# One expert-layer kernel: two of its weight blocks loaded in 16 transfers of eight partitions each

## The chip, the core and the metric

The kernel runs on one core of a Trainium2 chip. A core has TensorE (PE; its weight loads, PEld, overlap its matmuls), VectorE (DVE), ScalarE (ACT), GpSimd (POOL) and SyncE (SP). SP computes nothing here: it issues transfers between HBM and the on-chip memory of 128 partitions, which 16 DMA engines carry out. The metric is the device time of one execution in microseconds.

## What is computed

A layer over 256 latent tokens and 256 context tokens, all of width 1024: a token mixer (a recurrent part and a pooling part), then a mixture of 32 experts, of which each token takes four. Cut to what matters here:

```python
logits = (h @ router_w + router_b)
top_v, top_i = lax.top_k(logits, TOP_K)                # 4 of 32
...
for e in range(N_EXPERTS):
    gu = h @ w1[e] + b1[e]                             # (1024, 2048) float32
    glu = jnp.minimum(gu[:, :D_EXPERT], SWIGLU_LIMIT)
    lin = jnp.clip(gu[:, D_EXPERT:], -SWIGLU_LIMIT, SWIGLU_LIMIT)
    act = glu * jax.nn.sigmoid(SWIGLU_ALPHA * glu) * (lin + 1)
    out = out + gates[:, e:e + 1] * (act @ w2[e] + b2[e])   # w2[e]: (1024, 1024)
```

The two matrices of an expert are 8 MB and 4 MB of float32, so the 32 experts read 402.7 MB.

## The kernel before, in words

The first part (to about 210 us) is the mixer and the router. It sorts the experts by their number of tokens; what follows goes through them in that order, as places p = 0 to 31, experts 0 and 1 always first. Only the experts behind places 2 to 31 are found at run time: SP reads their number from `ord_i` (L106) and forms the address with it.

The tokens of an expert are gathered in groups of 32. `gemm1` (L860) multiplies one or two groups by the first matrix, L867, `swiglu` follows on DVE and ACT, `turn` (L900) transposes, and `gemm2` (L909) multiplies by the second matrix, L916. `combine` (L931) adds the result to the tokens. The second half of an expert runs after the first half of the next pass.

All large weights come as blocks of 1 MB, 128 partitions by 2048 elements: eight per first matrix (keys `("w1", p, 0)` to `("w1", p, 7)`, 128 rows of 8 KB each) and four per second matrix (keys `("w2", p, 0)` to `("w2", p, 3)`, two rows of 4 KB for each partition). `plan` (L67 to L124) is the order in which they are loaded: for each place its eight first blocks, then the four second blocks of the place before (L119 to L123). A block needs a slot. There are 12 at first, and the mixer gives eight of its buffers back when it is done with them (`donate`, L173), so that 20 blocks fit. `due` (L133) takes keys from the plan while slots are free, and `load` (L154) lets SP issue the transfers at L156, one after the other. `gemm1` and `gemm2` retire a block with its last use (`retire`, L161), which frees the slot for a later one; PE has to be through with it before SP may issue. One block of the mixer and the very last block are loaded in two halves (L148).

SP's order: each DMA of the program takes the next of eight semaphores, DMAHW0 to DMAHW7, and waits until the DMA that had it before has landed. At most eight transfers are therefore under way. A DMA into a block that PE used before waits for PE too. Who reads a block waits for the semaphores of the DMAs that filled it.

Some smaller transfers matter below: at the start ACT issues a table `ptab` to 64 partitions of 4 KB each (L266) beside SP's loads of the tokens to 128 partitions, and four one-partition rows `bgrow` (L276); SP loads the gate weights in two halves of 64 partitions (L281, at 34.6 us); at the end SP stores the result in four transfers of 256 KB (L1144).

Of the kernel before, what the change touches and what calls it, by code (L numbers as in the profile page):

```python
# [18 lines left out]
P = 128  # L19
# [37 lines left out]
def hybrid(tc, a, out):  # L57
# [8 lines left out]
    w_mod, w_in, w_out, w1, w2 = a["w_mod"], a["w_in"], a["w_out"], a["w1"], a["w2"]  # L66
# [26 lines left out]
    for q in (2, 3, 0, 1):  # L93
        src = w_out[256 * q : 256 * q + 256, :]
# [8 lines left out]
    def source(key):  # L103
        kind, p, j = key
        if p not in expert:
            expert[p] = nc.values_load(ord_i[0:1, p : p + 1], engines=[ENG.SP], min_val=0, max_val=NE - 1)  # L106
        return expert_source(kind, expert[p], j)
# [20 lines left out]
    def block(tag):  # L128
        if tag not in tiles:
            tiles[tag] = blocks.tile([P, 2048], F32, tag=tag, name="blk")  # L130
        return tiles[tag]

    def due():  # L133

        todo = []
        while plan and (plan[-1][0] in own or slots):
            key, src = plan.pop()
            if src is source:
                src = source(key)
            if key in own:  # L140
                t = own[key]
            else:
                tag = slots.pop(0)
                t = block(tag)
                if len(src.shape) == 3:
                    t = t.rearrange("p (k n) -> p k n", k=src.shape[1])
                live[key] = (t, tag)
            if key in (("mod", 1, 3), ("w2", NE - 1, 3)):  # L148
                todo += [(t[:, k], src[:, k]) for k in range(2)]
            else:  # L150
                todo.append((t, src))
        return todo

    def load(todo):  # L154
        for t, src in todo:
            sp.dma_start(t, src)  # L156

    def weight(*key):
        return live[key][0]

    def retire(*keys):  # L161

        todo = []
        for key in keys:
            slots.append(live.pop(key)[1])
            todo.append(due())
        return todo

    def free(*keys):
        for todo in retire(*keys):  # L170
            load(todo)

    def donate(*tags):  # L173
        slots.extend(tags)
        load(due())
# [29 lines left out]
    key = const.tile([P, NE], F32, name="key")  # L205
# [47 lines left out]
    with ExitStack() as px:  # L253
# [26 lines left out]
        for hh in range(2):  # L280
            r = slice(64 * hh, 64 * hh + 64)  # L281
            own[("gaw", hh)] = gaw[r, :, r]
            pool.memset(gaw[r, :, 64 * (1 - hh) : 64 * (1 - hh) + 64], 0.0)
        own[("poolw",)] = poolw
        load(due())


# [976 lines left out]
```

## Time and profile before

| | |
|---|---|
| median of 3 runs | 1105.54 us (1105.21 to 1105.77) |
| the profiled execution | 1105.46 us, its span 1103.8 us |
| granted PE clock, mean | 0.954 |
| busy | PE 980.9 us (89%), DVE 300.2, ACT 164.6, POOL 54.9 |
| read from HBM | 442.25 MB, 402 GB/s over the span |
| chain that ended last | PE 55%, DMA 42% |
| issue to landing of an expert's block | 19.6 us |

Busy shares are averages over stages. The slices tell the stages apart: a PE that is 89% busy may wait in just the places that set the end, and a DMA stream at a constant rate may be that rate's own limit or the limit of what it is asked. The waits tell which.

### The profile page before, as it was taken

Reading aid. Unit: us, or ns where it says so; the run is one execution under the profiler, and the core shown is the slowest. Engines: PE = TensorE matmul, PEld = TensorE weight load, DVE = VectorE, ACT = ScalarE, POOL = GpSimd, SP = SyncE. Lnnn points to the kernel's source line nnn. Section 1 sums busy time; section 2 is a strip of 40 time slices with the busy share of each in tenths; the row PEclk is TensorE's granted clock in tenths of the full one; section 3 lists DMA queues with packets and bytes.
Section 4 is the critical chain, followed back from the end, with each engine's and each line's share of the span. In section 5 each row is a group of like instructions: output and inputs, shape, how many; then the busy total and the mean of one; then the engine's idle time right before and its main releaser. Section 6 shows DMA issues by size and latency. Waiting matters only on the chain.

```text
span 1103.8 us, 21803 instructions
## 1 busy us (share of the span) xinstructions
PE 980.9 (89%) x9237; PEld 420.1 (38%) x9238; DVE 300.2 (27%) x803; ACT 164.6 (15%) x347; POOL 54.9 (5%) x73
## 2 busy tenths in 40 slices
PE   7899999999999968699998897969999887999774
PEld 3356654434444313243433242324343233444222
DVE  4436562231313211213312112212221221223114
ACT  3245342101111000101010010000101010110011
POOL 2128200000000000000000000000000000000001
PEclk9899999999999989989998998989999998999886
DMA  9999689999999999999999999999999999999993
GB/s 366 355 404 374 260 348 379 376 422 424 422 424 423 423 424 424 424 425 424 423 424 424 424 423 424 423 425 423 424 422 425 425 423 424 425 423 414 424 422 135
DMA packets 89861, 444.76 MB, mean 403 GB/s; under 512 B 9304, under 2 KB 15576, under 8 KB 56992
## 3 DMA queue, kind: packets, MB, share of 16 engines
q1 hardware_dynamic: 89528, 443.01, 97.4%
q8 instruction: 74, 1.21, 0.4%
q10 hardware_dynamic: 232, 0.32, 0.1%
q14 instruction: 27, 0.22, 0.1%
HBM read 442.25 MB, written 1.05 MB: 402 GB/s over the span
## 4 chain that ended last, share of the span: by engine, by line
PE 55%; DMA 42%; DVE 2%; ACT 0%; issue 0%; ACTq 0%; SPq 0%; DVEq 0%
DMA blk<-in_w_dram 40%; PE ph L867 22%; PE py L916 12%; PE zp L458 5%; PE misc L847 3%; DMA blk<-in_w_mod_dram 2%; PE acc L604 2%; PE acc L933 2%; PE ph L881 2%; PE gp L373 1%; PE acc L488 1%; PE misc L906 1%; PE bp L233 1%; DMA cols<-in_cols_dram 0%; PE misc L857 0%; PE acc L718 0%
## 5 line engine op out<-in xcount | busy, mean ns | idle before, releaser
L867 PE MATMUL ph<-blk,xe 128*32 128x512 f32 x3584 | 430.4, 612 | 40.1 <-DMA blk<-in_w_dram 38.9
L916 PE MATMUL py<-blk,aT 128*32 128x256 f32 x3584 | 221.8, 400 | 54.5 <-DMA blk<-in_w_dram 49.8
L867 PEld LDWEIGHTS ph<-blk,xe 128*32 128x32 f32 x3584 | 104.2, 111 | 281.5 <-issue 176.3
L916 PEld LDWEIGHTS py<-blk,aT 128*32 128x32 f32 x3584 | 117.0, 115 | 170.8 <-issue 56.6
L929 DVE TENSOR_TENSOR Y<-py,g2s 32x256 f32<-32x256 f32 x224 | 94.2, 420 | 232.1 <-PE py L916 229.3
L894 DVE TENSOR_SCALAR av<-ph 128x256 f32<-128x256 f32 x56 | 23.6, 422 | 463.6 <-PE ph L881 463.6
L907 ACT ACTIVATE aT<-misc 128x256 f32<-128x256 f32 (+1 forms) x38 | 18.4, 485 | 386.2 <-PE misc L906 386.2
L850 ACT ACTIVATE xe<-misc,AB 128x128 f32<-128x128 f32 x108 | 40.7, 457 | 167.9 <-PE misc L847 167.9
L847 PEld LDWEIGHTS misc<-Pm,blk 128*128 128x128 f32 x432 | 51.4, 195 | 23.8 <-issue 23.8
L458 PE MATMUL zp<-blk 128*128 128x256 f32 (+1 forms) x192 | 59.2, 465 | 1.1 <-DVE blk L425 1.1
L847 PE MATMUL misc<-Pm,blk 128*128 128x128 f32 x432 | 56.5, 285 | 1.1 <-DVE Pm L826 1.1
L881 PE MATMUL ph<-b,SM 128*32 128x512 f32 x448 | 56.8, 609 | 0.0
L895 ACT ACTIVATE sgm<-av 128x256 f32<-128x256 f32 x56 | 23.3, 417 | 212.1 <-DVE av L894 212.1
L933 PE MATMUL acc<-Y,PgT 128*128 128x512 f32 (+1 forms) x120 | 51.9, 576 | 0.5 <-DVE Y L929 0.5
L1139 POOL TENSOR_TENSOR blk<-blk 128x512 f32<-128x512 f32 (+1 forms) x2 | 2.0, 995 | 941.7 <-ACT blk L1138 940.9
L458 PEld LDWEIGHTS zp<-blk 128*128 128x128 f32 x192 | 37.1, 195 | 22.6 <-issue 17.6
L933 PEld LDWEIGHTS acc<-Y,PgT 128*128 128x128 f32 x120 | 21.4, 189 | 31.3 <-issue 21.9
L881 PEld LDWEIGHTS ph<-b,SM 128*32 128x32 f32 x448 | 15.0, 114 | 35.7 <-issue 35.7
L604 PE MATMUL acc<-blk 128*128 128x512 f32 x64 | 27.8, 592 | 0.0
L897 DVE SCALAR_TENSOR_TENSOR av<-l,av 128x256 f32<-128x256 f32 x56 | 23.8, 426 | 10.8 <-ACT sgm L895 9.6
L373 PE MATMUL gp<-blk,csil 128*32 128x256 f32 x384 | 22.6, 381 | 2.1 <-DMA blk<-in_w_mod_dram 2.1
L906 PEld LDWEIGHTS misc<-ident,av 128*128 128x128 f32 x112 | 11.9, 144 | 32.9 <-issue 32.1
(214 smaller groups left out, 459.6 us busy)
## 6 DMA issues: line engine op xcount, KB each, us to landing
blk<-in_w_dram SPq DMA_DIRECT2D x383, 1024.0 KB, 19.6
blk<-in_w_mod_dram SPq DMA_DIRECT2D x23, 1024.0 KB, 10.6
blk<-in_w_in_dram SPq DMA_DIRECT2D x6, 1024.0 KB, 16.0
blk<-in_w_out_dram SPq DMA_DIRECT2D x4, 1024.0 KB, 5.3
blk<-in_ctx_dram SPq DMA_DIRECT2D x2, 512.0 KB
blk<-in_x_dram SPq DMA_DIRECT2D x2, 512.0 KB
blk<-in_w_mod_dram SPq DMA_DIRECT2D x2, 512.0 KB, 16.2
blk<-in_w_dram SPq DMA_DIRECT2D x2, 512.0 KB
```

What stands on the lines that cost most here:

```text
L373: pe.matmul(gp[32 * c : 32 * c + 32, :], csil[:, k, :], w[:, kk, T * c : T * c + T], start=(k == 0), stop=(k == KD - 1), skip_group_check= ...
L458: pe.matmul(zp[:, :n], w[:, k, P * half : P * half + P], hT(k)[:, :n], start=(k == 0), stop=(k == KD - 1))
L604: pe.matmul(acc[h][half], mixT[:, k, P * h : P * h + P], weight("out", k // 2)[:, k % 2, 512 * half : 512 * half + 512], start=(k == 4), s ...
L847: pe.matmul(gx[:, kk], xn[:, t, P * k : P * k + P], Pm[:, t], start=(t == 0), stop=(t == 1))
L850: act.activation(xe[:, k], gx[:, kk], AF.Identity, bias=AB[:, 1, k : k + 1], scale=AB[:, 0, k : k + 1])
L867: pe.matmul(ph[32 * c : 32 * c + 32], x[:, k], wv[:, :, c, :], start=(k == 0), stop=False, skip_group_check=True,)
L881: pe.matmul(ph[32 * c : 32 * c + 32], sel[c].to_broadcast([P, GS]), b1, start=False, stop=True, skip_group_check=True,)
L894: dve.tensor_scalar(av, ph[:, 0, :], 7.0, None, op0=ALU.min)
L897: dve.scalar_tensor_tensor(av, l1, 8.0, av, op0=ALU.min, op1=ALU.mult)
L916: pe.matmul(py[32 * c : 32 * c + 32, i], aT[:, i, k % 2, k // 2, :], W[k // 2][:, k % 2, T * c : T * c + T], start=(k == 0 and i == 0), st ...
L929: dve.tensor_tensor(dst[:, T * c : T * c + T], py[r, i], g2s[r], op=ALU.mult)
L933: pe.matmul(acc[t][h][:, lo:hi], PgT[:, P * t : P * t + P], Y[:, 512 * h + lo : 512 * h + hi], start=False, stop=False, skip_group_check=True,
```

## The change

The first block of the first matrix at places 8 and 16 is loaded in 16 DMAs of eight partitions (64 KB) each, in the order of the partitions. All other blocks, and the order of the plan, stay as they are.

```diff
             if key in (("mod", 1, 3), ("w2", NE - 1, 3)):
                 todo += [(t[:, k], src[:, k]) for k in range(2)]
+            elif key in (("w1", 8, 0), ("w1", 16, 0)):
+                todo += pieces(t, src)
             else:
                 todo.append((t, src))
...
+    def pieces(t, src):
+
+        return [(t[8 * i : 8 * i + 8], src[8 * i : 8 * i + 8]) for i in range(P // 8)]
```

SP's instructions at the first of the two places, before: four second blocks of place 6 (128x2x1024), then the eight first blocks of place 8 (128x2048); the names in brackets are the semaphores that the DMA waits for.

```order
L156 DMA blk<-in_w_dram 128x2x1024 [waits DMAHW2_49,PE_49]
...
L156 DMA blk<-in_w_dram 128x2x1024 [waits DMAHW3_49,PE_49]
...
L156 DMA blk<-in_w_dram 128x2048 [waits DMAHW4_49,PE_49]
...
L156 DMA blk<-in_w_dram 128x2048 [waits DMAHW5_49,PE_49]
...
L156 DMA blk<-in_w_dram 128x2048 [waits DMAHW6_49,PE_49]
```

The same place in the changed kernel, where line 158 is line 156 of before. Between the first and the second row of pieces (8x2048) shown and the last one stand the others, 16 in all, each behind one `ISA` row.

```order
L158 DMA blk<-in_w_dram 128x2x1024 [waits DMAHW3_49,PE_49]
...
L158 DMA blk<-in_w_dram 8x2048 [waits DMAHW4_49,PE_49]
...
L158 DMA blk<-in_w_dram 8x2048 [waits DMAHW5_49]
...
L158 DMA blk<-in_w_dram 8x2048 [waits DMAHW3_49]
...
L158 DMA blk<-in_w_dram 128x2048 [waits DMAHW4_49,PE_49]
...
L158 DMA blk<-in_w_dram 128x2048 [waits DMAHW5_49,PE_49]
```

The piece on DMAHW3 waits for the last block of place 6, and the next whole block, on DMAHW4, stands behind all 16 and waits for a piece.

PE at the first matmuls that read the block, before: the last second block of the pass before, then the first two blocks of place 8.

```order
L916 MATMUL py<-blk,aT 32x256 [waits DMAHW3_49]
...
L867 MATMUL ph<-blk,xe 32x512 [waits DMAHW4_49]
L867 MATMUL ph<-blk,xe 32x512 x3
...
L867 MATMUL ph<-blk,xe 32x512 [waits DMAHW5_49]
```

And in the changed kernel:

```order
L922 MATMUL py<-blk,aT 32x256 [waits DMAHW3_49]
...
L873 MATMUL ph<-blk,xe 32x512 [waits DMAHW4_49,DMAHW5_49,DMAHW3_49,DMAHW6_49,DMAHW2_49,DMAHW7_49,DMAHW1_49,DMAHW0_49]
L873 MATMUL ph<-blk,xe 32x512 x3
...
L873 MATMUL ph<-blk,xe 32x512 [waits DMAHW4_49]
```

The first matmul waits for all eight semaphores in place of one; the rest of PE's order is as before.

## Rows read from the trace of the kernel before

**Rows 1.** The page's slices, 40 of 27.6 us: busy tenths, and what the DMAs moved.

```profile
PE   7899999999999968699998897969999887999774
DMA  9999689999999999999999999999999999999993
GB/s 366 355 404 374 260 348 379 376 422 424 422 424 423 423 424 424 424 425 424 423 424 424 424 423 424 423 425 423 424 422 425 425 423 424 425 423 414 424 422 135
```

**Rows 2.** Stretches from 215 to 1075 us: length, busy, clock, DMA share, GB/s.

```profile
core 0: us, PE busy (x) PEld busy (x) DVE busy (x) ACT busy (x) POOL busy (x), PEclk, DMA share, GB/s
...
215.00:340.00 125.00, 124.51 (x1378) 52.49 (x1374) 32.91 (x92) 13.67 (x33) 0.00 (x0) 1.00 1.00 415
340.00:365.00 25.00, 25.00 (x302) 11.91 (x295) 6.99 (x17) 2.72 (x7) 0.00 (x0) 1.00 1.02 423
365.00:580.00 215.00, 187.04 (x1886) 72.62 (x1878) 46.59 (x132) 20.13 (x49) 0.00 (x0) 0.95 1.02 424
580.00:605.00 25.00, 20.49 (x220) 8.78 (x216) 6.37 (x20) 1.92 (x5) 0.00 (x0) 0.89 1.02 424
605.00:1075.00 470.00, 409.91 (x4086) 158.19 (x4078) 98.30 (x272) 44.20 (x107) 0.00 (x0) 0.95 1.02 423
```

**Rows 3.** PE's waits: us in total, times, longest.

```profile
PE py L916 <- DMA blk<-in_w_dram: 49.8, 31, 10.5
PE ph L867 <- DMA blk<-in_w_dram: 38.9, 52, 1.6
```

**Rows 4.** Timeline near the end: start, length, what, and in brackets the idle time before.

```profile
1077.60 1.94 PE L916 MATMUL py<-blk,aT 128*32 128x256 f32 x16 [1.39 <-DMA blk<-in_w_dram]
```

**Rows 5.** SP's own waits: us in total, times, longest.

```profile
SPq L156 <- DMA blk<-in_w_dram: 403.5, 247, 3.2
SPq L156 <- PE ph L867: 112.1, 87, 6.4
```

**Rows 6.** The page's DMA issues: count, KB each, median us to landing.

```profile
blk<-in_w_dram SPq DMA_DIRECT2D x383, 1024.0 KB, 19.6
...
out_dram<-blk SPq DMA_DIRECT2D x4, 256.0 KB, 2.0
```

**Rows 7.** Line L156, from 100 us to 342.2 and to 581.8: ns, first and last start.

```profile
L156 SPq DMA_DIRECT2D blk<-in_w_dram x93: 327/367/4242, 104.5 to 342.2; - x93
...
L156 SPq DMA_DIRECT2D blk<-in_w_dram x189: 327/373/4242, 104.5 to 581.7; - x189
```

**Rows 8.** Line L156 from 215 to 222 us: ns min/median/max, first and last start.

```profile
L156 SPq DMA_DIRECT2D blk<-in_w_dram x4: 332/332/333, 215.6 to 220.8; - x4
L156 SPq FUSED_REGOPS  x4: 43/46/46, 216.0 to 221.8; - x4
L156 SPq EVENT_SEMAPHORE  x4: 17/17/17, 216.1 to 221.9; - x4
L156 SPq MOVE blk<-in_w_dram x4: 29/29/29, 216.2 to 221.9; - x4
```

**Rows 9.** Line L276, four transfers to one partition each.

```profile
L276 ACTq DMA_DIRECT2D bgrow<-in_bgrow_dram x4: 230/232/481, 5.4 to 7.7; - x4
```

**Rows 10.** The page's packets and instruction queues: packets, MB, share of 16 engines.

```profile
DMA packets 89861, 444.76 MB, mean 403 GB/s; under 512 B 9304, under 2 KB 15576, under 8 KB 56992
...
q8 instruction: 74, 1.21, 0.4%
...
q14 instruction: 27, 0.22, 0.1%
```

**Rows 11.** DMA rate from 1 to 9 us, 40 slices of 0.2 us.

```profile
GB/s 0 0 0 0 20 41 227 61 0 20 287 328 348 328 266 205 184 164 307 369 430 279 387 436 403 410 410 410 430 410 430 410 430 410 430 410 430 430 410 420
```

**Rows 12.** DMA rate from 33.5 to 39.5 us, 40 slices of 0.15 us.

```profile
GB/s 375 389 382 382 382 382 396 352 343 301 294 297 299 285 287 280 335 266 276 244 159 84 36 34 15 21 12 19 17 19 236 128 99 73 128 208 277 300 382 273
```

## The prediction, made before the changed kernel ran

> **What bounds the kernel now.** I read the page's slices first: from the ninth slice on the DMA engines are busy nine tenths or more, and the rate stands at 422 to 425 GB/s in nearly every slice, while PE has gaps [rows 1]. The stretches say the same in fewer numbers: 423 or 424 GB/s from 340 to 1075 us, while PE is busy 187.0 of 215 us and 20.5 of 25 [rows 2]. PE's own waits in the expert loop end with landings of weight blocks: 49.8 us at L916 and 38.9 us at L867 [rows 3], and so does the last expert's matmul at 1077.6 us [rows 4], after which only a fixed tail comes. So the stream of weights sets the end. A block is 1024 KB, at 424 GB/s 2.47 us, and each microsecond in which the stream does less is added to the end, unless it had been idle there before, which these stretches leave no room for.
>
> Then the queue. A block lands 19.6 us after its issue [rows 6]; divided by 2.47 that is eight blocks under way. SP's waits show what holds it there: 403.5 us in 247 waits for the landing of an earlier block, 112.1 us for PE [rows 5]. The order of SP says why: DMAs take eight semaphores (DMAHW0 to 7) in turn, and each waits until the DMA eight places before it has landed. The limit is eight transfers, whatever their size.
>
> **The change, part by part.** The two blocks are the 93rd and the 189th of the stream: issued at 342.2 and 581.7 us [rows 7], in stretches where the stream is full.
>
> 1. *The issue chain.* Piece 0 waits as the block did. Pieces 1 to 7 take the semaphores of the seven blocks ahead, one every 2.47 us, so they cost SP only waiting. Piece 7 goes out when the last whole block ahead has landed. By then everything else in the queue is pieces, and the next whole block stands nine issues behind. One issue by SP is the DMA instruction (332 ns) with a register operation of 46, a move of 29 and a semaphore event of 17 ns: 0.42 us busy [rows 8]. The four in that row are spaced wider because they wait. A DMA of one partition takes 230 ns [rows 9], which makes 0.305 us without the event, the lower end; 0.57 us, with gaps between the instructions as long as half of their work, is the upper. I take 0.45, nearer to the row of this line: 9 x 0.45 = 4.05 us. To that comes the idle time between the last data of the block ahead and its landing, and between an issue and its first data. Both together are in the store: 2.0 us from issue to landing for 256 KB [rows 6], less 0.62 us for the bytes at 424 GB/s, so 1.4 us. The engines that get no piece stand idle for 5.45 us, where before they moved a block in 2.47: 2.98 us lost for each block (1.7 to 4.1), 6.0 for both (3.4 to 8.2).
>
> 2. *The pieces themselves.* The page counts 89861 packets, 56992 of them under 8 KB [rows 10]: 32869 of 8 KB or more. The first matrices have 32 x 8 blocks of 128 rows of 8 KB, 32768 rows, and the two instruction queues add 74 and 27. So a row is one packet, and a piece is eight packets, which can occupy eight of the 16 engines at most. At 26.5 GB/s for an engine (424 / 16) a piece then takes at least 0.31 us. The upper end: in a whole block each partition receives its 8 KB in 2.47 us; were that the pace of the receiving partitions, a piece would take 2.47 us too. What tells between the ends is a load on half of the partitions, the 256 KB table on 64 of them at the start. From 3.0 to 5.0 us the ten slices average 279 GB/s, 557 KB, and then the rate goes to 410 to 430 with 128-partition loads alone [rows 11]. The 295 KB that are not the table take 0.70 us at 420 GB/s, which leaves 1.30 us for the table: 202 GB/s, half the rate for half the partitions. The two gate loads on 64 partitions each, at 34.6 us, also run at about 300 GB/s where 380 stood before [rows 12]; their packets are of 256 bytes, so this is weaker. So the receiving side has shares, and eight neighbours hold between one share in 16 (2.47 us) and eight (0.31 us). I take the middle on a scale of doublings, 0.875 us. [...]
>
> 3. *The sum.* Pieces 0 to 6 are queued ahead, so the engines that carry pieces work from the end of the block ahead for 16 x 0.875 = 14.0 us. That is more than the 5.45 us of the chain, which lies beside it. Lost are 14.0 - 2.47 = 11.5 us for each block, 23.1 for both. Something is given back: the engines with pieces lag, and others catch up on work of their own. PE's instruction queue holds 0.4% of 16 engines' time, 70.6 us [rows 10]; were all of it on the eight engines without pieces, the others would win back 8.8 us by the end, on the same eight nothing. I take half, 4.4.
>
> 4. *Small things.* The first matmul on a split block waits for eight semaphores in place of one, and three instructions near the end get four to six waits more: some 28 events of 17 ns [rows 8], 0.5 us, of which 0.1 us in the tail is on the path. PE runs dry while the pieces land, but it is idle 28 of the 215 us behind the first place and 60 of the 470 behind the second [rows 2], so it catches up.
>
> The profiled execution took 1105.46 us, 0.08 under the median of the runs. 1105.5 + 23.1 - 4.4 = 1124.2: **1124 us**.
>
> **The rivals.** *Only the chain counts* (0.32): eight neighbouring partitions receive as fast as eight engines send, or the rows of different pieces spread over the receiving side. Then 16 x 0.31 = 5.0 us hides behind the chain's 5.45, and the time is 1105.5 + 6.0 = 1111.5 (1109 to 1114). For it: the early table lies in the kernel's first microseconds, where a slow start may explain the dip. Against it: the rate falls after it had risen to 348 GB/s [rows 11].
>
> *The load moves to the engines that have room* (0.04), the case on the other side. If the instruction queue's 70.6 us lie on the eight engines that get no pieces, these set the landings, and each split block spares them 2.47 us: 1105.5 - 4.9 = 1100.6. [...] It decides only if the next block's data start within 2.47 us, so nine issues in 1.1 us, 0.12 each; the cheapest DMA in the trace takes 0.23 [rows 9]. That speaks nearly conclusively against it.
>
> *The cost is hidden* (0.04): the stall falls where the stream would have waited for PE, or the 16 pieces are queued as one. Then 1105.5. The 423 GB/s around both places [rows 2] speak against it.
>
> *The receiving side is slower still* (0.05): 2.47 us for a piece gives 39.5 us for a block, and 1105.5 + 74 = 1180. Two halves 64 partitions apart, as the gate loads are, would have to be the only shares.
>
> **How the numbers follow.** The forecast has 0.55: pieces between 0.65 and 1.24 us, so 1121 without anything given back at the low end, 1117 with it, and 1136 to 1140 at the high one. With the chain alone it makes 0.87; the range from 1109.5 to 1138 leaves out faster, hidden, the slowest receiving side and some of both edges, near 0.2. This kernel's runs tell 0.2%, 2.2 us, from no change. Slower by more than that: 0.55 + 0.32 + 0.05 = 0.92; the same 0.04; faster 0.04.
>
> **What would show it.** SP must show 32 pieces and, behind each group, eight or nine issues close together after a landing. Two holes in the rate must stand near 359 us and between 600 and 610: about 5 us at the level of none for half of the engines if the chain alone counts, 12 to 15 us far under 200 GB/s if the receiving side does. PE's waits for weight blocks must grow by about what the time grows. I am wrong if the rate shows no hole, if a hole is there and the end does not move, or if the holes are right and the later rate differs from 424 GB/s.

## The result: 1121 us, and the profile after

The changed kernel takes 1121.15 us (median of 4 runs, 1120.14 to 1121.89) against 1105.38 for the kernel before in the same session: 1.0147 times as long, 95% interval 1.0132 to 1.0163, 15.8 us slower. Forecast were 1124 and "slower". The profiled execution took 1121.33 us, its span 1119.7, 15.9 more than before. Lines of the program moved by two ahead of the new helper and by six behind it: L156 is L158, L867 is L873, L916 is L922.

The page's slices of the changed kernel (28.0 us each: busy tenths, then GB/s), to lay beside [rows 1]:

```profile
PE   7899999999999868789995887869989787999764
DMA  9999689999998999999998999999999999999993
GB/s 367 365 410 366 275 350 385 367 422 423 423 424 331 378 425 424 424 424 424 423 424 285 420 422 424 424 424 424 424 424 424 424 424 424 424 423 423 424 422 155
```

From the ninth slice to the last but one there are two places, three slices in all, under 420 GB/s: 331 and 378 near 350 us, 285 near 600. The stretches give the two places their size (columns as in [rows 2], other bounds):

```profile
340.00:375.00 35.00, 30.09 (x322) 13.12 (x314) 8.26 (x20) 2.72 (x7) 0.00 (x0) 0.90 0.85 315
375.00:580.00 205.00, 180.48 (x1822) 70.76 (x1818) 43.61 (x124) 19.50 (x48) 0.00 (x0) 0.93 1.02 424
580.00:620.00 40.00, 23.21 (x252) 9.03 (x248) 8.04 (x24) 2.52 (x6) 0.00 (x0) 0.93 0.88 326
620.00:1075.00 455.00, 394.65 (x4026) 154.47 (x4018) 96.68 (x268) 43.73 (x106) 0.00 (x0) 0.97 1.02 424
```

Missing are 35 x (1 - 315/424) = 9.0 us of the stream at the first place and 40 x (1 - 326/424) = 9.2 us at the second, 18.2 in all; between and behind them the rate is 424. The rate from 335 to 395 us and from 585 to 645 us in slices of 1.5 us shows the holes themselves:

```profile
GB/s 437 426 404 431 421 431 407 426 410 412 418 429 418 380 178 112 44 131 87 87 186 131 377 431 421 421 431 431 431 415 415 431 418 415 415 429 412 423 426 437
...
GB/s 437 415 421 437 415 418 421 421 421 423 415 358 172 153 87 82 109 98 131 186 257 437 415 421 437 421 415 431 437 421 431 396 423 423 410 421 418 421 437 431
```

Eight slices, 12 us, stand under 190 GB/s in each. Two short stretches within each hole (columns as above; the last two are the busy share of the 16 DMA engines, 1.02 in the full stream [rows 2], and GB/s):

```profile
358.00:361.00 3.00, 3.00 (x11) 1.09 (x13) 0.97 (x3) 0.24 (x1) 0.00 (x0) 1.00 0.22 79
362.00:365.00 3.00, 2.52 (x48) 1.26 (x40) 0.41 (x1) 0.00 (x0) 0.00 (x0) 1.00 0.51 87
...
606.00:608.00 2.00, 0.43 (x8) 0.29 (x12) 0.00 (x0) 0.00 (x0) 0.00 (x0) 1.00 0.19 78
609.00:613.00 4.00, 0.51 (x12) 0.02 (x4) 3.33 (x8) 0.00 (x0) 0.00 (x0) 1.00 0.54 111
```

In the later stretch of each hole the share, 0.51 and 0.54, is about that of eight engines out of 16, and they move 87 and 111 GB/s, a piece of 64 KB in 0.75 and 0.59 us. They were not short of work then. SP's instructions on L158 from 359.5 to 364.6 us (ns min/median/max, first and last start) are pieces 7 to 15 and the next whole block:

```profile
L158 SPq DMA_DIRECT2D blk<-in_w_dram x10: 277/277/371, 359.6 to 364.3; - x10
L158 SPq FUSED_REGOPS  x9: 46/46/51, 360.0 to 364.1; - x9
```

Nine steps in 4.7 us are 0.52 us each, the last of them longer for the whole block's wait; 64 KB in 0.52 us would be 126 GB/s. In the earlier stretch of each hole the share is 0.22 and 0.19, less than half of what eight busy engines show: most engines had run dry, so pieces 0 to 6 must have been largely through, and SP was still waiting for the landing that lets piece 7 out, at 359.6 us in the first hole and 607.5 in the second. The page's packets, beside [rows 10], tell how many engines had a part in a piece:

```profile
DMA packets 90086, 444.77 MB, mean 397 GB/s; under 512 B 9528, under 2 KB 15800, under 8 KB 57216
```

Those under 512 bytes grew by 224. In the kernel before 2898 of them came with 189.8 MB, 181 blocks, from 620 to 1070 us, 16 for each block. One for each engine and transfer gives just the 224 with eight engines for a piece and 16 for a whole block: 32 x 8 - 2 x 16.

PE's and SP's waits, beside [rows 3] and [rows 5]:

```profile
PE py L922 <- DMA blk<-in_w_dram: 56.9, 33, 11.0
PE ph L873 <- DMA blk<-in_w_dram: 51.4, 52, 7.2
```
```profile
SPq L158 <- DMA blk<-in_w_dram: 429.7, 263, 3.1
SPq L158 <- PE ph L873: 110.4, 78, 6.0
```

PE waits 108.3 us for weight blocks where it waited 88.7, 19.6 more, and SP 26.2 us more for landings, but no more for PE: the transfers are late, and PE is not. The end of the stream shows where 2.3 of the 18.2 us went. The first row is the changed kernel's rate from 1076 to 1101 us, in slices of 0.625 us:

```profile
GB/s 413 419 413 433 419 413 419 419 400 419 413 419 426 426 419 426 419 426 419 426 419 387 406 419 413 426 426 419 419 426 413 387 315 288 262 262 256 236 229 210
```

and the second the kernel before, from 1060 to 1085 us:

```profile
GB/s 433 419 419 433 413 419 419 419 419 419 419 413 419 426 419 419 419 426 419 419 419 426 419 400 406 419 419 367 275 269 262 262 229 249 249 236 216 210 210 210
```

The fall from the full rate begins with 367 at 1076.9 us before (the 28th value) and with 387 at 1095.4 now (the 32nd): 18.5 us later, what the holes took to within a slice. The end of the span came only 15.9 us later. So the tail at about half of the rate, in which a part of the engines has nothing left (share 0.60 from 1077 to 1085 us before and 0.66 from 1095.4 to 1101 us now, against 1.02 ahead of it), became 2.3 us shorter by the holes, 2.6 by these rows.

### The profile page after: what moved, and what is told of

Its sections match the earlier page's. It is cut to its first block, busy times and chain, and to the rows that moved or that the text cites. A ratio compares the mean times of both kernels' runs of the same rounds, so it can differ in the third digit from the quotient of the medians.

```text
span 1119.7 us, 21908 instructions
## 1 busy us (share of the span) xinstructions
PE 975.4 (87%) x9237; PEld 417.4 (37%) x9238; DVE 299.9 (27%) x803; ACT 164.5 (15%) x347; POOL 54.9 (5%) x73
## 4 chain that ended last, share of the span: by engine, by line
PE 55%; DMA 42%; DVE 1%; SPq 1%; issue 0%; ACT 0%; ACTq 0%; DVEq 0%
DMA blk<-in_w_dram 39%; PE ph L873 22%; PE py L922 11%; PE zp L464 5%; PE misc L853 3%; PE acc L939 3%; PE ph L887 3%; DMA blk<-in_w_mod_dram 2%; PE acc L610 2%; PE gp L379 1%; PE acc L494 1%; PE misc L912 1%; SPq L158 1%; DMA cols<-in_cols_dram 0%; PE misc L863 0%
## 5 line engine op out<-in xcount | busy, mean ns | idle before, releaser
L873 PE MATMUL ph<-blk,xe 128*32 128x512 f32 x3584 | 430.0, 611 | 54.6 <-DMA blk<-in_w_dram 51.4
L922 PE MATMUL py<-blk,aT 128*32 128x256 f32 x3584 | 219.4, 397 | 61.6 <-DMA blk<-in_w_dram 56.9
L873 PEld LDWEIGHTS ph<-blk,xe 128*32 128x32 f32 x3584 | 104.5, 111 | 297.1 <-issue 188.3
L922 PEld LDWEIGHTS py<-blk,aT 128*32 128x32 f32 x3584 | 116.0, 114 | 175.8 <-issue 55.2
L904 DVE TENSOR_TENSOR av<-av,sgm 128x256 f32<-128x256 f32 x56 | 23.8, 425 | 1.9
```

What stands on the lines that cost most here:

```text
L873: pe.matmul(ph[32 * c : 32 * c + 32], x[:, k], wv[:, :, c, :], start=(k == 0), stop=False, skip_group_check=True,)
L904: dve.tensor_tensor(av, av, sgm, op=ALU.mult)
L922: pe.matmul(py[32 * c : 32 * c + 32, i], aT[:, i, k % 2, k // 2, :], W[k // 2][:, k % 2, T * c : T * c + T], start=(k == 0 and i == 0), st ...
```

## The experiments

All kernels are the changed kernel with the edit shown, unless the text says otherwise. Each was timed beside the kernel before in its own session (1104.3 to 1105.7 us).

**Sixteen pieces of every fourth partition.**

```diff
-        return [(t[8 * i : 8 * i + 8], src[8 * i : 8 * i + 8]) for i in range(P // 8)]
+        return [(t[32*q+r : 32*q+32 : 4], src[32*q+r : 32*q+32 : 4]) for q in range(4) for r in range(4)]
```

> The same two blocks, the same 16 transfers of eight partitions, but every fourth partition of 32 in place of eight neighbours. Theory A (neighbouring partitions share their intake; the packets of the change took about 0.74 us in place of 0.31): the packets go back to about 0.31 us, what is left is the issue chain with its 3 us per block, about 1111.5 us. Theory B (small transfers on half of the engines are slow whatever partitions they go to): as the change, 1121 us.

Measured: 1122.08 us, ratio 1.0146 [1.0129, 1.0163], as slow as the change. It does not decide, since the edit changed a second thing. SP's instructions from 359 to 367.4 us, the same ten as above:

```profile
L158 SPq DMA_DIRECT2D blk<-in_w_dram x10: 355/644/664, 359.1 to 367.1; - x10
```

Issuing eight partitions that are not neighbours takes 644 ns in place of 277, and the nine steps 8.0 us in place of 4.7. Its rate from 335 to 395 us:

```profile
GB/s 410 442 421 426 421 421 431 418 407 410 426 412 429 421 385 199 27 87 87 87 49 87 213 421 415 421 437 437 431 410 421 426 421 426 401 429 415 423 423 421
```

And its stretch from 360 to 367 us (columns as for the stretches above):

```profile
360.00:367.00 7.00, 4.49 (x67) 2.05 (x65) 1.67 (x4) 0.00 (x0) 0.00 (x0) 0.99 0.28 77
```

Here 77 GB/s is what SP gives out (64 KB in 0.89 us are 74), and the share of 0.28 says that the eight engines stood idle for nearly half of the time. A longer chain took the place of slow rows. The shares do tell something of the rows: for each GB/s the engines were busy 0.28 / 77 here, against 0.51 / 87 and 0.54 / 111 in the change, an estimate of 0.62 to 0.75 of its time for the same bytes. The pieces also came further apart here, so that this is a sign and not a proof.

**Eight pieces of 16 partitions, neighbours and every eighth.**

```diff
-        return [(t[8 * i : 8 * i + 8], src[8 * i : 8 * i + 8]) for i in range(P // 8)]
+        return [(t[16 * i : 16 * i + 16], src[16 * i : 16 * i + 16]) for i in range(P // 16)]
...
+        return [(t[i::8], src[i::8]) for i in range(8)]
```

> Eight transfers of 16 neighbouring partitions for each of the two blocks: all 16 engines can take part, and with eight transfers the next whole block waits for the first piece alone, so no chain of issues behind a landing. Theory A: a piece of 128 KB still goes into few shares, 0.74 to 1.2 us each, so 5.9 to 9.8 us for a block of 2.47: 1112 to 1120 us. Theory B (half of the engines and the chain made the cost): both are gone, 1105.5 to 1107 us.

> As the run with eight transfers of 16 partitions, but every eighth partition of 128 in place of 16 neighbours. Theory A: the cost of that run goes away, 1105.5 to 1107 us. Theory B: no difference between the two.

Measured: 1114.78 us, 1.0078 [1.0061, 1.0095], for neighbours, 1114.22, 1.008 [1.0063, 1.0097], for every eighth: the same, about 4.5 us a block. Their rates from 585 to 645 us, neighbours first:

```profile
GB/s 421 418 429 412 418 423 421 423 421 210 180 194 137 197 197 344 426 431 431 437 399 426 431 410 437 426 412 421 418 418 426 404 440 442 415 421 431 415 437 415
```
```profile
GB/s 404 429 426 410 421 426 418 421 442 216 202 175 183 208 218 415 421 421 415 426 415 437 431 431 437 391 410 431 421 415 421 418 421 437 415 437 431 431 437 421
```

Only one issue of a piece stands behind the last whole block here, so the chain is nearly gone, and still the stream falls to half of its rate, 137 to 218 GB/s, for 9 us. By the packets all 16 engines have a part in each piece: with every eighth partition those under 512 bytes grew by 224 over the kernel before, one for each engine and transfer (16 x 16 - 2 x 16), and from 585 to 645 us either run has 469 of them. I read this as evidence against sharing by neighbours, and looked for a price of small transfers. The next runs speak against an equal price for each small transfer; why these two kinds of piece cost the same they do not tell.

**Sixteen and eight pieces of all partitions.** Transfers of 64 KB again, cut by columns, so that every engine and every partition has its share of each; then eight of 128 KB, at seven places (4, 8, ... 28) instead of two.

```diff
+        return [(t[:, 128 * i : 128 * i + 128], src[:, 128 * i : 128 * i + 128]) for i in range(16)]
...
-            elif key in (("w1", 8, 0), ("w1", 16, 0)):
+            elif key in [("w1", p, 0) for p in range(4, NE, 4)]:
...
+        return [(t[:, 256 * i : 256 * i + 256], src[:, 256 * i : 256 * i + 256]) for i in range(8)]
```

> 16 transfers for each of the two blocks again, but each over all 128 partitions and 128 columns (512 bytes a row). The chain of issues stands, eight neighbours and half of the engines are gone. Theory A: only the chain, 3 us per block, about 1111.5 us. Theory B with the number of transfers as its cause: as the change, 1121 us.

> The same seven blocks in eight transfers of all 128 partitions by 256 columns (128 KB in rows of 1 KB). Sixteen such transfers of 128 columns cost 5.6 us a block. If that is the chain (nine issues between the landing of the last whole block and the next whole one, while the queue holds only small transfers), eight transfers put one issue there and cost 0 to 0.7 us a block: 1105.5 to 1110.5. If it is a price of each small transfer (5.6 / 16 = 0.35 us each), eight cost 2.8 us a block: about 1125.

Measured: 1116.71 us, 1.0102 [1.0085, 1.0119], with 16, which is 5.6 us a block; 1116.16, 1.0097 [1.008, 1.0114], with eight at seven places, 10.9 / 7 = 1.55 us a block. The difference of eight issues is 4.05 us, 0.51 each. Eight transfers cost more than the 0.7 us a block expected of the chain, and less than the 2.8 us that an equal price for each transfer would make. SP's ten instructions with 16 columns, from 357.8 to 363.4 us, and the rate from 335 to 395:

```profile
L158 SPq DMA_DIRECT2D blk<-in_w_dram x10: 332/333/337, 357.9 to 363.1; - x10
```
```profile
GB/s 431 399 421 437 426 431 426 401 412 418 421 421 421 387 269 92 131 129 92 127 426 415 410 437 426 431 426 426 410 431 426 399 421 429 412 426 418 431 440 415
```

Nine steps in 5.2 us, 0.58 each. Between them, from 358 to 363 us, the engines are busy for 0.41 at 110 GB/s:

```profile
358.00:363.00 5.00, 5.00 (x61) 2.42 (x63) 0.26 (x1) 0.00 (x0) 0.00 (x0) 1.00 0.41 110
```

That is 64 KB in 0.60 us, what SP gives out. So this is the issue chain alone, and it follows the number of issues behind the last whole block, as the prediction has it. But it is longer than forecast. The hole is worth 6.2 us of the full stream; with the 2.5 us that the block itself takes the engines were without whole blocks for 8.6 us, of which the issues are 5.2 and the latencies 3.4 us, where 1.4 was forecast. The row shows a part of the reason: the rate is down to 387 and 269 from 354.5 to 357.5 us, before piece 7 went out at 357.9. I read this as the block ahead landing only with its last engine, when others have run dry; the rows do not show single engines.

**Eight small pieces and a half, two halves, and even and odd partitions,** at the seven places.

```diff
+        return [(t[8*i : 8*i+8], src[8*i : 8*i+8]) for i in range(8)] + [(t[64:], src[64:])]
...
+        return [(t[q+r : q+32 : 4], src[q+r : q+32 : 4]) for q in (0, 32) for r in range(4)] + [(t[64:], src[64:])]
...
+        return [(t[:64], src[:64]), (t[64:], src[64:])]
...
+        return [(t[0::2], src[0::2]), (t[1::2], src[1::2])]
```

> At seven places (4, 8, ... 28) the first block goes out as eight transfers of eight neighbouring partitions and one of the other 64: nine transfers, so that hardly any issue chain is left (two issues more than a queue of eight holds, about 1 us beyond the one that the block took). All theories count against the kernel before, 1105.5 us. Theory N (neighbouring partitions share an intake): a piece takes 0.74 us as in the steady part of the changed kernel's hole, eight of them 5.9 us on eight engines, with 1.2 us for the half 7.1 in place of 2.5 us: 4.6 us a block, 32 in all, about 1135 (1125 to 1140). Theory S (an engine with a single row in a transfer is slow, wherever the row goes): the same 1135, and the run with every fourth partition is as slow. [...]

> The same seven blocks, nine transfers and sizes, but each piece takes every fourth partition of 32 (eight of them, spread over the first 64), then the other 64 in one. SP's issue of such a piece was 0.84 us where one of neighbours was 0.47, which here hides behind the queue. Theory N: pieces at 0.31 us, at most 1.2 us a block: 1105.5 to 1114, some 20 us under the run with neighbours. Theory S: as slow as that run, about 1135. [...]

> The control for the two runs with eight pieces: the same seven blocks in two transfers of 64 partitions. [...] If the two halves run one after the other at half of the rate, as the early 64-partition table did (202 GB/s), a block takes 5.2 us and 2.7 us is lost: 1124. If the engines mix them with their neighbours in the queue, nothing is lost: 1105.5 to 1107. The second is the likelier, as the transfers around them are of 128 partitions and no engine waits.

> The seven blocks of the run with halves, in two transfers of 64 partitions again, but the even partitions and then the odd ones. The halves cost 7.1 us a block, 49.5 in all. Theory N (each group of neighbouring partitions has its intake, and half of the intakes give half of the rate): the even partitions reach all groups, so nothing is lost: 1105.5 to 1108. Theory X (a transfer that doesn't give each engine the partitions that it has in a 128-partition transfer slows the whole stream to about 200 GB/s as long as one engine is in it): as slow as the halves, 1140 to 1160.

Measured: 1141.86 us, 1.0342 [1.0303, 1.0382], with eight neighbours; 1133.44, 1.0245 [1.0226, 1.0264], with every fourth; 1154.77, 1.0442 [1.0413, 1.0471], with two halves; 1106.09, 1.0005 [0.9995, 1.0015], with even and odd partitions. The control was the surprise. Two transfers of 64 neighbours cost 7.1 us a block, more than the 5.2 and 4.0 us of the nine transfers, and the same two transfers of every second partition cost nothing. The rates where such a block is loaded, first the halves from 725 to 785 us, then even and odd partitions from 335 to 395 us:

```profile
GB/s 404 429 415 421 426 298 246 202 246 314 284 229 221 249 235 257 251 229 306 388 431 410 437 426 426 412 401 426 421 418 399 415 396 429 437 423 429 434 431 426
```
```profile
GB/s 437 421 404 421 431 431 415 418 410 415 423 423 426 434 448 404 415 421 431 415 437 437 431 431 421 404 421 412 415 423 421 421 426 429 429 431 437 426 426 410
```

There is no hole at all with even and odd partitions, and one of 21 us at 202 to 314 GB/s with halves. The engines were busy throughout that hole (share 1.03), so the transfers were slow and not late:

```profile
732.00:753.00 21.00, 13.86 (x124) 4.85 (x120) 3.27 (x9) 0.83 (x2) 0.00 (x0) 0.87 1.03 258
```

Number and size of the transfers and of their rows are the same; what differs is which partitions receive together (and with them, which of the same 128 rows are read together). So it is the neighbourhood that costs, of the receiving partitions or of the rows that are read: every edit here cuts both alike, and no run parts them. The two mixed runs agree in sign, every fourth partition cheaper by 8.4 us, but each also holds a half of 64, so that they price neither piece.

**The pieces between whole blocks.** Block 7 of places 8 and 16 is cut instead of block 0, its slot is taken first, and two or three pieces follow each of the other seven blocks. The aim was that the queue is never left with pieces alone. Three cuts: eight neighbours as in the change, every fourth partition, and 128 columns.

```diff
-            plan += [(("w1", p, k), source) for k in range(KD)]
+            plan += [(("w1", p, k), source) for k in ([7] + list(range(7)) if p in (8, 16) else range(KD))]
...
-            elif key in (("w1", 8, 0), ("w1", 16, 0)):
-                todo += pieces(t, src)
+            elif key in (("w1", 8, 7), ("w1", 16, 7)):
+                todo.append((pieces(t, src), None))
...
+            if src is None:
+                pending.extend(t)
+                continue
             sp.dma_start(t, src)
+            for _ in range(min(len(pending), 3 if len(pending) > 12 else 2)):
+                sp.dma_start(*pending.pop(0))
```

> At places 8 and 16 the same 16 pieces of eight neighbours, of block 7 instead of block 0, put two or three at a time behind each of the seven whole blocks of the same place. The queue then always holds whole blocks, so that SP's nine issues lie beside data: no chain. Chain theory (all of the 15.7 us come from the nine issues with a queue of small transfers, and the slow 8 KB packets too): 1105.5, 1103 to 1107.5. Chain and rows (5.2 us a block from the chain, 2.7 from rows that run slower): 1109 to 1112. If eight engines carry 16 rows of a block and the others none, and the eight with the rows are those that are late at the end, up to 2.5 us a block more; if they are the early ones, up to 2.5 us a block less than before: 1100.6 at the least.

> As the run with the pieces between whole blocks, each piece of every fourth partition. [...] If that run shows no cost, none here either; SP's longer issue (0.84 us) fits beside the 2.5 us of a block only twice, so up to 0.2 us a piece, 6 us in all, could come from it where three pieces stand together: 1105.5 to 1108 as the likelier.

> As the run with the pieces between whole blocks, but each of the 16 transfers of block 7 takes all 128 partitions by 128 columns, 64 KB as before. The number and size of the transfers, their order and the eight semaphores are the same; every engine and every partition gets an equal share. If what the pieces between whole blocks cost (21 us) comes from the rows' place (eight partitions, eight engines), nothing is left: 1105.5 to 1107.5, and no hole in the rate at 350 to 390 us. If it comes from small transfers that take up the eight places in the queue, the 21 us stay: 1120 to 1127. Rows of 512 bytes may take somewhat longer than a share of one of 8 KB: the sixteen column transfers kept 25 to 27 ns a row where 8192 / 512 of one took 19, so up to 1 us a block.

Measured: 1126.74 us, 1.0196 [1.0182, 1.021], with neighbours; 1119.5, 1.0122 [1.0105, 1.0139], with every fourth; 1108.53, 1.0037 [1.0023, 1.005], with columns. The rates from 335 to 395 us in this order:

```profile
GB/s 426 415 426 426 437 437 401 421 401 415 423 426 418 431 442 289 328 289 175 382 279 246 317 421 213 306 350 229 257 328 251 246 268 298 380 344 429 423 415 448
```
```profile
GB/s 426 437 404 437 421 431 407 423 404 412 429 421 415 434 434 426 393 328 229 426 339 404 333 328 339 268 300 366 262 243 325 273 333 377 426 418 423 434 431 423
```
```profile
GB/s 437 421 426 421 426 421 421 418 399 429 421 418 423 431 416 419 391 268 339 401 206 367 387 443 388 448 380 434 376 422 415 426 423 412 429 440 410 437 426 431
```

I had half expected the cost to go with the chain. It rose, from 15.8 to 21.1 us. At this first place the hole is shallower and 30 us long, while whole blocks and pieces lie in the queue together. At the second place the aim was missed. With neighbours the engines had little to do for 4 us:

```profile
610.00:614.00 4.00, 2.61 (x40) 0.97 (x36) 2.49 (x6) 0.00 (x0) 0.00 (x0) 1.00 0.32 94
```

Between its whole blocks at 601.0 and 612.8 us SP gave out three pieces, at 603.4, 606.3 and 609.4, each after a wait for a landing: a slow piece holds one of the eight places in the queue as a whole block does. With columns, where number, size, order and semaphores of the transfers are the same, 4.2 us are left. So 17 of the 21 us are the price of eight rows on eight neighbouring partitions, with the waits that they bring, and 7.2 of these go with every fourth partition, where they are no neighbours. With every fourth partition 9.6 us are left above the columns. Of these an engine that carries 16 rows of the block in place of eight may take 2.5 us a block; what the rest is was not tried.

## Why the prediction was right, point by point

**What bounds the kernel** held: what is missing from the stream, 18.2 us, moved the end of its full rate by 18.5, a slice of 0.6 us being the accuracy.

**1. The issue chain** was there as described, nine issues after the landing of the last whole block, but under-sized: 5.45 us of idle engines were forecast, 8.6 us stand in the run with 16 column transfers. The issue term was 4.05 and measured 4.7 in the change (5.2 there). The latency term is what failed: 1.4 us, taken from four stores at the end of the kernel [rows 6], measured 3.4. A store that runs alone was no measure of that latency in a loaded queue.

**2. The pieces** were the right choice between the two rivals, and over-sized: 0.875 us a piece, the middle of a wide scale, where the stretches with about eight busy engines say 0.75 and 0.59. The reason given, that the receiving side has shares and neighbours fall into few of them, is shown in part. Neighbours cost more in the halves against the even and odd partitions, 49.5 us against none, and between whole blocks, 21.1 us against 13.8 with every fourth partition. But 9.6 us more than the columns' 4.2 came with eight rows that are no neighbours, of which 5.0 may be the load on eight engines, and 16 neighbours cost no more than every eighth partition. So a rival for a part of the price was left untested: that an engine with a single row in a transfer is slow wherever the row goes. And that it is the receiving side, and not the reading of neighbouring rows, is argued. The number that set the choice, 202 GB/s for an early table on 64 partitions [rows 11], has no clean counterpart: the hole of the halves, 258 GB/s on average, carried whole blocks as well.

**3. The sum** holds a step that failed: that pieces 0 to 6 keep their engines at work from the end of the block ahead, so that chain and pieces lie beside each other and the longer one counts. The shares of 0.22 and 0.19 show the engines dry before piece 7 went out. The rate broke at 356.0 and 603.0 us, and piece 7 left 3.6 and 4.5 us later; the nine pieces from there on came behind this wait, not beside it. An estimate: 3.6 us and nine pieces of 0.75 make 10.4 us at the first place, 4.5 us and nine of 0.59 make 9.8 at the second, of the 11.6 us that the stream was without whole blocks (9.1 lost and the block's own 2.5). The forecast had 14.0 there, all of it pieces: its latency of 1.4 us was shorter than the seven pieces queued ahead, so that no wait came into the sum. That the same eight engines carry every piece, as 16 x 0.875 takes it, no row shows; the shares of 0.51 and 0.54 are those of about eight busy at a time. Lost were 9.1 us a block, not 11.5. Given back were 2.3 us of the forecast 4.4, at the end of the stream; that this was the instruction queue's work, and that the queue is PE's, no row shows. 1105.5 + 18.2 - 2.3 = 1121.4 is no second check on the 1121.33, since the 2.3 is what the span leaves of the 18.2. The forecast came within about 3 us with two errors of 5 and 2 us, of opposite sign, and with a wait missing that dearer pieces made up for: its nearness is partly luck.

**4. Small things** need no correction: PE lost its time with the transfers, and its waits for weight blocks grew by 19.6 us with the time's 15.9. That they grew more was not forecast; PE was busy 5.5 us less (975.4 us of 980.9).

**The rivals.** That only the chain counts (1111.5) was wrong in its premise and too small in its price; the chain alone made 1116.7. That the load moves to engines with room was not seen: no run was faster than the kernel before. The slowest receiving side (2.47 us a piece) would have shown a floor of 27 GB/s.

What stays open: why halves cost 7.1 us a block. Half of the rate for the two transfers alone is 2.5 us. The hole of the halves was about 4.5 us of stream at the first of the seven places, 230 to 260 us in slices of 0.75 us,

```profile
GB/s 431 410 404 410 415 437 421 404 426 169 158 158 197 208 229 229 208 186 251 218 382 448 371 459 404 470 393 437 426 415 448 382 448 393 470 393 437 426 415 459
```

and 8.5 us at 732 to 755 us. So transfers of whole blocks beside the halves are slow as well, and later in the kernel for longer. That engines drift apart during the kernel, and the two halves are then in work over a longer time, is only argued. Open too are why neighbours and every eighth partition cost the same in pieces of 16, what a single row for each engine costs by itself, and whether neighbours cost in receiving or in reading. A run that reads neighbouring rows into partitions far apart would part the last two.

## What to carry to other kernels

Cut a transfer so that each part still reaches all neighbourhoods of partitions (columns, or every second partition): the same two transfers cost 0 or 7.1 us a block. Where a fixed number of transfers may be under way, count the issues that stand behind the last large one; each beyond the limit cost about half a microsecond of a stream of 424 GB/s, and the latency before it must be read under load. Look at the engines' busy share before calling two delays parallel: here they had run dry between them. An edit that is meant to take one stall away can bring another: with the pieces between whole blocks the cost rose from 15.8 to 21.1 us.

## What the runs showed of the hardware that I had not expected

Narrow transfers of neighbours slowed others: with two halves of 64 the whole stream ran at 202 to 314 GB/s for 21 us, though the halves are 1 MB, which the full rate moves in 2.5 us, and the engines were busy throughout. SP's DMA instruction depends on the partitions: 277 ns for eight neighbours, 333 for all 128, 644 for eight at every fourth. And 32 transfers of 64 KB in place of two of 1 MB cost only 4.2 us where they stood between large ones and reached all partitions.
